# One row of each partition is read with the second load and the last, and one exponential makes its sum

## The chip, the cores and the metric

The kernel runs on one core of a Trainium2 chip. The metric is the device time of one execution in microseconds: 161.43 us as the median of 3 runs (161.34 to 161.46). The profile is one further execution, which took 161.56 us; its span, from the first to the last instruction recorded, is 160.2 us.

## The reference

The input `x` is 32 x 512 x 1024 in fp32 (67.1 MB), of normally distributed numbers. For each of the 16,384 rows of 1024 numbers the result is the logarithm of the sum of their exponentials:

```python
max_x = np.max(x, axis=-1, keepdims=True)
return max_x.squeeze(-1) + np.log(np.sum(np.exp(x - max_x), axis=-1))
```

## The kernel before

The kernel first computes `log(sum(exp(x)))` without taking the maximum off. It then counts whether any sum lies outside 1e-15 to 1e15, and only in that case does everything again with the maximum, inside `nc.If`. With this input that branch isn't taken.

**Rows.** Each of 128 partitions has NC = 128 rows. Rows 0 to 111 (W = 112) of a partition are neighbours in memory (`x_rows`: from one partition to the next it is 112 x 4 KB = 448 KB). The other B = 16 rows come from the end of the input (`x_rest`: 64 KB from one partition to the next). The order of reading is `x_rows`, then `x_rest`.

**Loads.** The list `LOADS` (L22) has 19 loads, counted from 0 here; each entry has its rows for each partition (they need not be whole) and what is done with them. SP issues all of them in order on one queue, into a ring of 48 rows in SBUF (`load`, L137). A load is issued when the sums that read its place in the ring are done. A load that no longer fits starts at the ring's beginning. The first is hoisted to the program's top (`start_early`).

**Work.** ACT waits for a load and writes its exponentials in place (L231), one instruction for each part of the entry. Then come the letters of the list:
- `R9`: DVE sums 9 rows in one reduction (L242).
- `G5`: POOL adds the second half of each of 5 rows to the first (L237); with a later `H`, DVE sums the half rows (`sum_folded`, L161).
- `T4`: DVE sums 4 rows one by one, each with an instruction that adds its halves and accumulates (`add_halves`, L169). At load 15 (`HELD`) DVE also waits for load 16's landing.
- `C`: DVE takes least and total of the sums so far, for the check at the end (`check_early`, L178).
- `L`: ACT takes the early logarithm, of the first 112 sums (L204).
- `a`, `b`: the last row comes in two loads. Part `a` (0.53 row) is added up by DVE into column 127 of `sumexp`; part `b` (480 elements) gets an exponential on ACT that itself accumulates its sum into `rest` (L226).

**End.** SP stores the 112 early results (L265). ACT takes the logarithm of the other 15 whole rows (L269), and then that of the last row, with `rest` as input and DVE's sum as the bias operand (L271). For the latter it waits for the semaphore `parts_summed`, which both parts raise. Then ACT copies `rest` into `sumexp` (L274), SP stores 16 results (L276), DVE checks the sums since `C` (L280, L284), TensorE adds the counts over the partitions in three small matmuls (L290 to L294), the last of them with ACT's copy, and DVE compares (L298). ACT and DVE read that flag and branch. SP waits for both branches and both stores, and ends.

The order of work on each engine is the order in which the Python code issues it, so the list sets it.

Of the kernel before, what the change touches and what calls it, by code (L numbers as in the profile page):

```python
# [11 lines left out]
B = 16  # L12
# [7 lines left out]


LOADS = [  # L22
# [5 lines left out]
]  # L28
# [25 lines left out]
def kernel(  # L54
# [29 lines left out]

    def source(e0, size):
        assert e0 >= W * d or e0 + size <= W * d
        return x_rest[:, e0 - W * d : e0 - W * d + size] if e0 >= W * d else x_rows[:, e0 : e0 + size]

    loads = [
# [5 lines left out]
    assert sum(size for size, _ in loads) == NC * d  # L95

    def sbuf(name, cols, dtype=fp32, rows=P):
        return nc.alloc_sbuf_tensor(name, [rows, cols], dtype).ap()
# [3 lines left out]

    LEAST, TOTAL, REST = NC, NC + 1, NC + 2
    sumexp = sbuf("sumexp", NC + 3)
    res = sbuf("res", NC)
    clamped = sbuf("clamped", NC)
# [5 lines left out]
    count = nc.alloc_psum_tensor("count", [1, 1], fp32).ap()  # L112
    rest = nc.alloc_psum_tensor("rest", [P, 1], fp32).ap()

    unused = nc.alloc_psum_tensor("unused", [P, H], fp32).ap()

    landed = [nc.alloc_semaphore(f"landed{i}") for i in range(len(loads))]
# [7 lines left out]
    ready = nc.alloc_semaphore("ready")  # L125

    parts_summed = nc.alloc_semaphore("parts_summed")
    stored = nc.alloc_semaphore("stored")
# [8 lines left out]
    def load(i, here, done_before, size):  # L137
        for a, b, who, at in users:
            if a < here + size and b > here:
                sp.wait(who, at)  # L140
        assert not any(p0 < here + size and p0 + s * d > here for _, p0, s, _ in folded)
        users[:] = [u for u in users if not (u[0] < here + size and u[1] > here)]
        return nc.sync.dma_start(  # L143
            out=ring[:, here : here + size], in_=source(done_before, size)
        ).then_inc(landed[i], 16)

    c = 0
# [9 lines left out]
    def sum_folded():  # L157
        for c0, p0, s, at in folded:
            dve.wait(pool, at)
            half = ring[:, p0 : p0 + s * d].rearrange("p (c d) -> p c d", d=d)[:, :, 0:H]  # L160
            at = dve.did(nc.vector.reduce_sum(out=sumexp[:, c0 : c0 + s], in_=half, axis=AX.X))  # L161
# [4 lines left out]
    def add_halves(v, col):  # L166
        h = v.shape[-1] // 2
        lo = v[:, 0:h]
        return nc.vector.scalar_tensor_tensor(  # L169
            out=lo, in0=lo, scalar=1.0, in1=v[:, h : 2 * h],  # L170
            op0=ALU.mult, op1=ALU.add, accum_out=sumexp[:, col : col + 1],
        )

# [7 lines left out]

    for i, (size, parts) in enumerate(loads):
        if here + size > RING * d:
            assert here == p
            p = here = 0
        dma = load(i, here, done_before, size)
        first_load = first_load or dma.ins
        end = here + size
        done_before += size
        act.wait(landed[i], 16)  # L190
        for k, part in enumerate(parts):
# [8 lines left out]
            if part[0][0] == "L":  # L200
                assert c >= W
                assert dve.seen[act.sem.num] >= summed_by_act
                act.wait(dve, max(at for c0, _, at in summed if c0 < W))
                ln_early = act.did(nc.scalar.activation(  # L204
                    out=res[:, 0:W], in_=sumexp[:, 0:W], func=AF.Ln
                ))
                continue
# [16 lines left out]
            v = ring[:, here:upto]  # L224
            if part[-1][0] == "b":
                nc.scalar.activation(  # L226
                    out=unused[:, 0 : upto - here], in_=v, func=AF.Exp, accum_out=rest
                ).then_inc(parts_summed, 1)
                here = upto
                continue  # L230
            at = act.did(nc.scalar.activation(out=v, in_=v, func=AF.Exp))  # L231
            here = upto
            for how, s in part:
                rows = ring[:, p : p + s * d].rearrange("p (c d) -> p c d", d=d)
# [5 lines left out]
                elif how == "R":  # L240
                    dve.wait(act, at)
                    users.append((p, p + s * d, dve, dve.did(nc.vector.reduce_sum(  # L242
                        out=sumexp[:, c : c + s], in_=rows, axis=AX.X
                    ))))
                    summed.append((c, c + s, dve.n))
                elif how == "T":
                    if i == HELD:
                        nc.vector.wait_ge(landed[i + 1], 16)
                        nc.vector.nop(nofuse=True)
                    dve.wait(act, at)  # L250
                    for r in range(s):
                        n_sums = dve.did(add_halves(rows[:, r, :], c + r))
                        users.append((p + r * d, p + (r + 1) * d, dve, n_sums))
                        summed.append((c + r, c + r + 1, n_sums))
                elif how == "a":
                    dve.wait(act, at)
                    add_halves(ring[:, p:upto], LAST).then_inc(parts_summed, 1)
                    s = 0
# [4 lines left out]
    assert by_act + sum(c1 - c0 for c0, c1, _ in summed) == LAST  # L263
# [5 lines left out]
    act.did(nc.scalar.activation(out=res[:, W:LAST], in_=sumexp[:, W:LAST], func=AF.Ln))  # L269
    nc.scalar.wait_ge(parts_summed, 2)  # L270
    ln_last = act.did(nc.scalar.activation(  # L271
        out=res[:, LAST:NC], in_=rest, func=AF.Ln, bias=sumexp[:, LAST:NC]
    ))
    last = act.did(nc.scalar.copy(out=sumexp[:, REST : REST + 1], in_=rest))  # L274
    sp.wait(act, ln_last)
    nc.sync.dma_start(out=out_rest, in_=res[:, W:NC]).then_inc(stored, 16)  # L276

    dve.wait(act, summed_by_act)
    nc.vector.wait_ge(parts_summed, 2)
    bads = dve.did(nc.vector.scalar_tensor_tensor(  # L280
# [13 lines left out]
    at = pe.did(nc.tensor.matmul(  # L294
        count, lhsT=ones, rhs=sumexp[:, REST : REST + 1], start=False, stop=True
    ))
# [9 lines left out]
    with nc.If(all_fine < 1):  # L306

        nc.scalar.wait_ge(sp.sem, 16)
        nc.scalar.wait_ge(stored, 16)
# [42 lines left out]
    nc.sync.wait_ge(done, 2)  # L352
    nc.sync.wait_ge(sp.sem, 16)
    nc.sync.sem_clear(range(landed[0].num, stored.num))
# [55 lines left out]
```

## Time and profile before

| | |
|---|---|
| median of 3 runs | 161.43 us |
| the profiled execution | 161.56 us |
| its span | 160.2 us |
| DVE busy | 116.1 us, 72% |
| ACT busy | 114.5 us, 71% |
| POOL busy | 33.3 us, 21% |
| read from memory | 67.11 MB, 419 GB/s over the span |
| exponentials (L231) | 25 of them, 112.2 us |
| row sums on DVE (L242, L161, L169) | 89.8, 16.5 and 9.8 us |

In the lines that follow, L242 is line 242 of the kernel before. A line of the timeline gives start and length in us, engine, line, operation, tiles, shapes and count; a bracket at its end gives how long the engine stood idle before it and what ended that. Neighbours of one kind may be merged, and the length is then theirs together. A group's line ends with busy us, mean ns of one, and idle us before. A line of the DMA issues ends with KB and the us from issue to landing. SPq is SP's queue of issues.

### The profile page before, as it was taken

Reading aid. Unit: us, or ns where it says so; the run is one execution under the profiler, and the core shown is the slowest. Engines: PE = TensorE matmul, PEld = TensorE weight load, DVE = VectorE, ACT = ScalarE, POOL = GpSimd, SP = SyncE. Lnnn points to the kernel's source line nnn. Section 1 sums busy time; section 2 is a strip of 40 time slices with the busy share of each in tenths; the row PEclk is TensorE's granted clock in tenths of the full one; section 3 lists DMA queues with packets and bytes.
Section 4 is the critical chain, followed back from the end, with each engine's and each line's share of the span. In section 5 each row is a group of like instructions: output and inputs, shape, how many; then the busy total and the mean of one; then the engine's idle time right before and its main releaser. Section 6 shows DMA issues by size and latency. Waiting matters only on the chain.

```text
span 160.2 us, 183 instructions
## 1 busy us (share of the span) xinstructions
PE 0.3 (0%) x6; PEld 0.2 (0%) x6; DVE 116.1 (72%) x56; ACT 114.5 (71%) x32; POOL 33.3 (21%) x14
## 2 busy tenths in 40 slices
PE   0000000000000000000000000000000000000000
PEld 0000000000000000000000000000000000000000
DVE  0000000029998499999999799929989999999996
ACT  3000069970899519992799449964998999999996
POOL 0000000000000000000000000990580489996000
DMA  8999799799699699997999999997999999999992
GB/s 288 479 511 431 336 514 450 321 514 497 272 512 512 288 463 478 478 448 312 424 467 467 467 429 429 429 429 332 498 426 409 415 440 394 438 419 425 417 408 101
DMA packets 3025, 67.18 MB, mean 419 GB/s; under 512 B 592, under 2 KB 720, under 8 KB 1488
## 3 DMA queue, kind: packets, MB, share of 16 engines
q1 hardware_dynamic: 3024, 67.18, 97.9%
q14 instruction: 1, 0.01, 0.0%
HBM read 67.11 MB, written 0.07 MB: 419 GB/s over the span
## 4 chain that ended last, share of the span: by engine, by line
DMA 54%; DVE 21%; ACT 19%; POOL 5%; issue 0%; PE 0%; SPq 0%
DMA ring<-in_x_dram 54%; ACT ring L231 19%; DVE sumexp L242 15%; POOL ring L237 5%; DVE ring L169 3%; DVE sumexp L161 2%; SPq L143 0%; DVE clamped L280 0%; PE count L290 0%; ACT res L204 0%; DVE fine L298 0%; PE count L292 0%; PE count L294 0%
## 5 line engine op out<-in xcount | busy, mean ns | idle before, releaser
L231 ACT ACTIVATE ring<-ring 128x16000 f32<-128x16000 f32 (+24 forms) x25 | 112.2, 4546 | 42.8 <-DMA ring<-in_x_dram 42.8
L242 DVE TENSOR_REDUCE sumexp<-ring 128x9 f32<-128x9216 f32 (+7 forms) x10 | 89.8, 9000 | 39.2 <-ACT ring L231 39.2
L237 POOL TENSOR_TENSOR ring<-ring 128x2048 f32<-128x2048 f32 (+5 forms) x8 | 33.0, 4135 | 112.3 <-ACT ring L231 112.3
L161 DVE TENSOR_REDUCE sumexp<-ring 128x4 f32<-128x2048 f32 (+5 forms) x8 | 16.5, 2080 | 3.5 <-POOL ring L237 3.5
L169 DVE SCALAR_TENSOR_TENSOR ring<-ring 128x512 f32<-128x512 f32 (+1 forms) x16 | 9.8, 671 | 0.0
L130 ACT ACT_TABLE_LOAD x1 | 1.3, 1283 | 1.4 <-PEq L63 1.4
L169 DVE DVE_READ_ACCUMULATOR ring<-ring 128x1 f32 x16 | 1.3, 82 | 0.0
L226 ACT ACTIVATE unused<-ring 128x480 f32<-128x480 f32 x1 | 0.6, 559 | 0.0
L290 PE MATMUL count<-far,bad 128*1 128x1 f32 x2 | 0.2, 164 | 158.7 <-DVE clamped L280 158.7
L178 DVE TENSOR_REDUCE sumexp<-sumexp 128x1 f32<-128x106 f32 x2 | 0.4, 258 | 0.0
L298 DVE TENSOR_SCALAR fine<-count 1x1 int32<-1x1 f32 x1 | 0.1, 146 | 0.3 <-PE count L294 0.3
L131 POOL MEMSET ones<- 128x1 f32 x1 | 0.1, 98 | 1.0 <-POOLq L63 1.0
L290 PEld LDWEIGHTS count<-far,bad 128*1 128x1 f32 x2 | 0.1, 80 | 158.7 <-DVE clamped L280 158.7
L204 ACT ACTIVATE res<-sumexp 128x112 f32<-128x112 f32 x1 | 0.3, 279 | 0.0
L271 ACT ACTIVATE res<-rest,sumexp 128x1 f32<-128x1 f32 x1 | 0.3, 261 | 0.0
L280 DVE SCALAR_TENSOR_TENSOR clamped<-sumexp 128x23 f32<-128x23 f32 x1 | 0.2, 183 | 0.0
L269 ACT ACTIVATE res<-sumexp 128x15 f32<-128x15 f32 x1 | 0.2, 205 | 0.0
L292 PE MATMUL count<-total,ones 128*1 128x1 f32 x2 | 0.2, 164 | 0.0
L294 PE MATMUL count<-sumexp,ones 128*1 128x1 f32 x2 | 0.2, 164 | 0.0
L284 DVE TENSOR_REDUCE total<-sumexp 128x1 f32<-128x24 f32 x1 | 0.2, 173 | 0.0
L274 ACT COPY sumexp<-rest 128x1 f32<-128x1 f32 x1 | 0.2, 152 | 0.0
L394 POOL MEMSET const-float32-0.0<- 128x1 f32 x1 | 0.1, 98 | 0.2 <-issue 0.2
(8 smaller groups left out, 0.8 us busy)
## 6 DMA issues: line engine op xcount, KB each, us to landing
ring<-in_x_dram SPq DMA_DIRECT2D x1, 8048.0 KB, 39.1
ring<-in_x_dram SPq DMA_DIRECT2D x1, 8016.0 KB, 57.6
ring<-in_x_dram SPq DMA_DIRECT2D x1, 8000.0 KB, 21.5
ring<-in_x_dram SPq DMA_DIRECT2D x1, 7472.0 KB, 25.8
ring<-in_x_dram SPq DMA_DIRECT2D x1, 7312.0 KB, 22.9
ring<-in_x_dram SPq DMA_DIRECT2D x1, 6720.0 KB, 21.5
ring<-in_x_dram SPq DMA_DIRECT2D x1, 5200.0 KB, 17.6
ring<-in_x_dram SPq DMA_DIRECT2D x1, 3584.0 KB, 19.1
```

Of the source, the lines that this page charges most:

```text
L130: nc.scalar.preload_act_table_set("natural_log_exp_and_others")
L161: at = dve.did(nc.vector.reduce_sum(out=sumexp[:, c0 : c0 + s], in_=half, axis=AX.X))
L169: return nc.vector.scalar_tensor_tensor(out=lo, in0=lo, scalar=1.0, in1=v[:, h : 2 * h], op0=ALU.mult, op1=ALU.add, accum_out=sumexp[:, co ...
L178: dve.did(nc.vector.tensor_reduce(out=sumexp[:, col : col + 1], in_=sumexp[:, 0:c], op=op, axis=AX.X))
L204: ln_early = act.did(nc.scalar.activation(out=res[:, 0:W], in_=sumexp[:, 0:W], func=AF.Ln))
L226: nc.scalar.activation(out=unused[:, 0 : upto - here], in_=v, func=AF.Exp, accum_out=rest).then_inc(parts_summed, 1)
L231: at = act.did(nc.scalar.activation(out=v, in_=v, func=AF.Exp))
L237: folded.append((c, p, s, pool.did(nc.gpsimd.tensor_tensor(out=rows[:, :, 0:H], in0=rows[:, :, 0:H], in1=rows[:, :, H:d], op=ALU.add,))))
L242: users.append((p, p + s * d, dve, dve.did(nc.vector.reduce_sum(out=sumexp[:, c : c + s], in_=rows, axis=AX.X))))
L269: act.did(nc.scalar.activation(out=res[:, W:LAST], in_=sumexp[:, W:LAST], func=AF.Ln))
L271: ln_last = act.did(nc.scalar.activation(out=res[:, LAST:NC], in_=rest, func=AF.Ln, bias=sumexp[:, LAST:NC]))
L290: pe.did(nc.tensor.matmul(count, lhsT=bad, rhs=far, start=True, stop=False))
```

## The change

The reading order is turned round: first `x_rest` (16 rows), then `x_rows` from the middle of its row 15 to its end, and last `x_rows` from its beginning up to that point. So row 15 of each partition's `x_rows` is split: its second part of 544 elements (`EARLY`) stands at the head of load 1, and its first part of 480 elements (`TAIL`) is the whole of load 18, the last.

- DVE sums the 544 early exponentials into column W = 112 of `sumexp`; later rows move up a column (`column`). The early logarithm `L` covers 113 columns and writes into `edge`, with that logarithm at the end of them.
- The last load no longer goes to the ring but to the places of `edge` right behind that logarithm. SP issues it after the early logarithm, with its wait. One exponential over 481 elements (the logarithm and the 480 numbers) then accumulates the whole row's sum into `whole`. The last logarithm has that alone as input, with no bias operand, and waits for ACT itself.
- The row before it, row 14 of `x_rows`, is read in the two loads before the last. Part `c` (0.5625 row) is added up by DVE into `in_part_sum`, part `a` (0.4375 row) by a DVE instruction that hasn't been used before in this kernel, `tensor_tensor_reduce`, with `in_part_sum` as its start value. The logarithm of 15 rows waits for it.
- The list has new cuts. Again there are 19 loads. The first three hold 16, 15.625 and 15.906 rows, the last 480 elements as before. POOL folds 25 rows in place of 29. `C` moves from load 8 to load 3.
- The early results go out in two stores in place of one (16 and 96 results), behind the last load in SP's queue.

```diff
 LOADS = [
-    (15.625, "R15"), (15.71875, "R16"), (15.65625, "R9 R7"), (14.59375, "R14"),
-    (14.28125, "G7 H R7"), (13.125, "G5 H R9"), (10.15625, "G4 H R3+G3 H"), (7, "G4 R2 H G1"),
-    (5.84375, "H C G2+R1 G3 H"), (4.46875, "T4"), (3.09375, "T3 L"), (2.40625, "T2"),
-    (1.75, "T2"), (1.25, "T1"), (0.75, "T1"), (0.65625, "T1"), (0.625, "T1"), (0.53125, "a"),
-    (0.46875, "b"),
+    (16, "R16"), (15.625, "R15"), (15.90625, "R16"), (15.21875, "C R15"), (15.8125, "R10 G6 H"),
+    (12.96875, "R7 G6"), (9.25, "R5 G4 H"), (7.25, "G4 R3 H"), (4.5, "G3 H G1 H G1 H"),
+    (4.125, "T4"), (2.96875, "T3 L"), (2.3125, "T2"), (1.71875, "T2"), (1.25, "T1"),
+    (0.9375, "T1"), (0.6875, "T1"), (0.5625, "c"), (0.4375, "a"), (0.46875, "b"),
 ]
...
+    def pieces(e0, size):
+        for start, end, at in (
+            (0, B * d, x_rest),
+            (B * d, W * d + EARLY, x_rows[:, (B - 1) * d + TAIL : W * d]),
+            (W * d + EARLY, NC * d, x_rows[:, 0 : (B - 1) * d + TAIL]),
+        ):
+            if start <= e0 and e0 + size <= end:
+                return at[:, e0 - start : e0 - start + size]
...
+    edge = sbuf("edge", B - 1 + W + 1 + TAIL)
+    early = edge[:, B - 1 : B + W]
...
             at = act.did(nc.scalar.activation(out=v, in_=v, func=AF.Exp))
             here = upto
+            if head is not None:
+                dve.wait(act, at)
+                sums = dve.did(nc.vector.reduce_sum(
+                    out=sumexp[:, W : W + 1], in_=ring[:, head : head + EARLY], axis=AX.X
+                ))
...
+                elif how == "c":
+                    dve.wait(act, at)
+                    in_part = add_halves(ring[:, p:upto], in_part_sum)
...
                 elif how == "a":
+                    dve.wait(dve, in_part)
                     dve.wait(act, at)
-                    add_halves(ring[:, p:upto], LAST).then_inc(parts_summed, 1)
+                    sums = dve.did(nc.vector.tensor_tensor_reduce(
+                        out=lo, in0=lo, in1=ring[:, middle + h : upto], scale=1.0, scalar=in_part_sum,
+                        op0=ALU.add, op1=ALU.add, accum_out=sumexp[:, LAST : LAST + 1],
+                    ))
...
     sp.wait(act, ln_early)
-    nc.sync.dma_start(out=out_rows, in_=res[:, 0:W]).then_inc(sp.sem, 16)
+    nc.sync.dma_start(
+        out=edge[:, B + W : B + W + TAIL], in_=pieces(done_before, TAIL)
+    ).then_inc(landed[-1], 16)
+    nc.sync.dma_start(out=out_rest, in_=early[:, 0:B]).then_inc(sp.sem, 16)
+    nc.sync.dma_start(out=out_rows[:, B:W], in_=early[:, B:W]).then_inc(sp.sem, 16)
+    act.wait(landed[-1], 16)
+    in_whole = act.did(nc.scalar.activation(
+        out=unused[:, 0 : TAIL + 1], in_=edge[:, B + W - 1 : B + W + TAIL], func=AF.Exp,
+        accum_out=whole,
+    ))
 
     sums = dve.n
     act.wait(dve, sums)
-    act.did(nc.scalar.activation(out=res[:, W:LAST], in_=sumexp[:, W:LAST], func=AF.Ln))
-    nc.scalar.wait_ge(parts_summed, 2)
-    ln_last = act.did(nc.scalar.activation(
-        out=res[:, LAST:NC], in_=rest, func=AF.Ln, bias=sumexp[:, LAST:NC]
-    ))
-    last = act.did(nc.scalar.copy(out=sumexp[:, REST : REST + 1], in_=rest))
+    act.did(nc.scalar.activation(out=late[:, 0 : B - 1], in_=sumexp[:, W + 1 : NC], func=AF.Ln))
+    act.wait(act, in_whole)
+    ln_last = act.did(nc.scalar.activation(out=late[:, B - 1 : B], in_=whole, func=AF.Ln))
+    last = act.did(nc.scalar.copy(out=sumexp[:, WHOLE : WHOLE + 1], in_=whole))
```

More of the change, by code (lines that the diff above doesn't have):

```diff
@@ L202 @@
                 assert dve.seen[act.sem.num] >= summed_by_act
-                act.wait(dve, max(at for c0, _, at in summed if c0 < W))
+                act.wait(dve, max(at for c0, _, at in summed if c0 <= W))
                 ln_early = act.did(nc.scalar.activation(
-                    out=res[:, 0:W], in_=sumexp[:, 0:W], func=AF.Ln
+                    out=early, in_=sumexp[:, 0 : W + 1], func=AF.Ln
                 ))
@@ L224 @@
             v = ring[:, here:upto]
[L225 to L230, printed above, removed]
             at = act.did(nc.scalar.activation(out=v, in_=v, func=AF.Exp))
             here = upto
+            if head is not None:
[3 more added lines that the diff above has]
+                ))
+                users.append((head, head + EARLY, dve, sums))
+                summed.append((W, W + 1, sums))
+                head = None
             for how, s in part:
```

64 lines of the change are left out of this document (42 added, 22 removed).

## The prediction

> **What bounds the kernel now.** I read the page's DMA lines first.
>
> ```profile
> span 160.2 us, 183 instructions
> ...
> q1 hardware_dynamic: 3024, 67.18, 97.9%
> ```
>
> One queue moves all 67 MB, and its packets fill 97.9% of sixteen engines' span. The chain of waits shows where that stream ends the run and where it does not (start, length, what):
>
> ```profile
> 119.72 23.78 DMA ring<-in_x_dram
> 143.50 0.02 issue
> 143.52 6.75 ACT ring L231 x2
> ...
> 156.74 1.74 DVE ring L169 x7
> ```
>
> Up to 143.50 the chain is loads and what frees their space; behind it stand ACT and then DVE. But the last loads belong beside them. The issues of the last two from SP's timeline (start, length), and from the DMA issues the times to landing of the last two loads and the two stores:
>
> ```profile
> 134.59 4.56 SPq L143 DMA_DIRECT2D ring<-in_x_dram  x1
> 139.19 3.71 SPq L143 DMA_DIRECT2D ring<-in_x_dram  x1
> ```
>
> ```profile
> ring<-in_x_dram SPq DMA_DIRECT2D x1, 272.0 KB, 22.6
> ring<-in_x_dram SPq DMA_DIRECT2D x1, 240.0 KB, 18.6
> out_dram<-res SPq DMA_DIRECT2D x1, 56.0 KB, 7.5
> out_dram<-res SPq DMA_DIRECT2D x1, 8.0 KB, 1.4
> ```
>
> 134.59 + 22.6 = 157.2 and 139.19 + 18.6 = 157.8. The end, from the timelines of ACT, DVE and SP:
>
> ```profile
> 155.99 1.92 ACT L231 ACTIVATE ring<-ring 128x672 f32<-128x672 f32 x3
> 157.82 0.56 ACT L226 ACTIVATE unused<-ring 128x480 f32<-128x480 f32 x1
> 158.31 0.13 ACT L226 ACTIVATION_READ_ACCUMULATOR unused<-ring 128x1 f32 x1
> 158.36 0.20 ACT L269 ACTIVATE res<-sumexp 128x15 f32<-128x15 f32 x1
> 158.50 0.26 ACT L271 ACTIVATE res<-rest,sumexp 128x1 f32<-128x1 f32 x1
> 158.66 0.15 ACT L274 COPY sumexp<-rest 128x1 f32<-128x1 f32 x1
> ```
>
> ```profile
> 158.01 0.44 DVE L169 SCALAR_TENSOR_TENSOR ring<-ring 128x272 f32<-128x272 f32 x1
> 158.38 0.08 DVE L169 DVE_READ_ACCUMULATOR ring<-ring 128x1 f32 x1
> ```
>
> ```profile
> 158.78 0.34 SPq L276 DMA_DIRECT2D out_dram<-res  x1
> ```
>
> Three things meet within 0.1 us: the last load lands at 157.8, ACT leaves the exponential before it at 157.91, and the last exponential starts at 157.82 (two of ACT's instructions overlap by some 0.09). DVE's share of the last row is summed at 158.46, ACT's at 158.44; the last logarithm (L271) needs both. Its store leaves at 158.78 and needs 1.4 us: 160.2, the span. So the time is the stream (157.8) plus 2.4 us of tail. The profiled execution took 161.56 us, 0.13 above the median of 161.43; I sum differences against it and take them off the median.
>
> **The stream.** Bytes and number of loads (19) stay. ACT's timeline gives its pace, by the exponentials that start as their load lands (loads 3, 4, 5, 6, 8, 9), and SP's the issue of load 6:
>
> ```profile
> 77.09 12.66 ACT L231 ACTIVATE ring<-ring 128x14944 f32<-128x14944 f32 x1 [3.98 <-DMA ring<-in_x_dram]
> 94.34 12.48 ACT L231 ACTIVATE ring<-ring 128x6560 f32<-128x6560 f32 x2 [4.60 <-DMA ring<-in_x_dram]
> 110.25 11.50 ACT L231 ACTIVATE ring<-ring 128x4224 f32<-128x4224 f32 x2 [3.42 <-DMA ring<-in_x_dram]
> 122.53 15.22 ACT L231 ACTIVATE ring<-ring 128x4096 f32<-128x4096 f32 x5 [0.79 <-DMA ring<-in_x_dram]
> 138.08 5.28 ACT L231 ACTIVATE ring<-ring 128x2912 f32<-128x2912 f32 x2 [0.33 <-DMA ring<-in_x_dram]
> 143.52 4.02 ACT L231 ACTIVATE ring<-ring 128x4576 f32<-128x4576 f32 x1 [0.16 <-DMA ring<-in_x_dram]
> ```
>
> ```profile
> 104.89 0.33 SPq L143 DMA_DIRECT2D ring<-in_x_dram  x1
> ```
>
> Load 4 has 14.28 rows a partition and took 94.34 - 77.09 = 17.25 us, 1.208 a row. The last 16 rows took 157.8 - 138.08 = 19.7 us, 1.23 a row: 0.4 us more than 16 x 1.208. I put that on the ten small loads' own cost, since 5.44 us for the 4.47 rows of load 9 is still 1.217. The same sum then holds with the new cuts: the last load again lands at 157.8, if the queue never runs dry.
>
> It runs dry when a load is issued after the one ahead of it has landed. Load 6 has the least room now: issued at 104.89, while load 5 lands at 110.25, 5.4 us ahead. For the new list I need durations, from the groups by form of single engines in short stretches (last columns: busy us, mean ns, idle before), and one row of POOL's timeline:
>
> ```profile
> L242 DVE TENSOR_REDUCE sumexp<-ring 128x16 f32<-128x16384 f32 x1 | 17.2, 17220 | 2.9 <-ACT ring L231 2.9
> L242 DVE TENSOR_REDUCE sumexp<-ring 128x1 f32<-128x1024 f32 x1 | 1.2, 1208 | 0.0
> L169 DVE SCALAR_TENSOR_TENSOR ring<-ring 128x512 f32<-128x512 f32 x1 | 0.7, 692 | 0.0
> L169 DVE SCALAR_TENSOR_TENSOR ring<-ring 128x272 f32<-128x272 f32 x1 | 0.4, 437 | 0.0
> L231 ACT ACTIVATE ring<-ring 128x16000 f32<-128x16000 f32 x1 | 13.5, 13536 | 18.8 <-DMA ring<-in_x_dram 18.8
> L226 ACT ACTIVATE unused<-ring 128x480 f32<-128x480 f32 x1 | 0.6, 559 | 0.0
> L271 ACT ACTIVATE res<-rest,sumexp 128x1 f32<-128x1 f32 x1 | 0.3, 261 | 0.0
> L269 ACT ACTIVATE res<-sumexp 128x15 f32<-128x15 f32 x1 | 0.2, 205 | 0.0
> L237 POOL TENSOR_TENSOR ring<-ring 128x512 f32<-128x512 f32 x1 | 1.3, 1274 | 0.0
> ```
>
> ```profile
> 143.44 3.44 POOL L237 TENSOR_TENSOR ring<-ring 128x1536 f32<-128x1536 f32 x1 [0.29 <-ACT ring L231]
> ```
>
> ACT: (13536 - 559)/15520 = 0.836 ns an element and 0.16 us each (0.18 for the small ones: three of 672, 640 and 544 fill 155.99 to 157.91, 1.92 = 1856 x 0.836 ns + 0.37, so each adds some 0.1 to its elements, overlap taken off). DVE sums: (17220 - 1208)/15360 = 1.042 ns and 0.14. Row by row at 1.208, loads 0 to 6 now land at 22.0, 40.9, 60.1, 78.5, 97.6, 113.3, 124.4. Load 3 needs the space of R16: 22.0 + 13.9 (exp) + 17.2 (sum) = 53.1, and load 2 lands at 60.1, 7.0 ahead. Load 4 needs R15: exp until 54.4, half row (0.7) and sum (16.2): 71.3 against 78.5. Load 5: R16 from 73.9 to 91.2 against 97.6. Load 6: R15 until 107.9 against 113.3, 5.4 ahead. Load 7: R10 until 118.6 against 124.4. Later loads are over 14 ahead. No margin is under the present smallest, so the new half-row sum (0.7 us) and the early check, which moves here from load 8 (two sums over 47 columns, 0.4 us), cost nothing; what hides them is this 5 to 7 us of queued transfers, past which they would cost in full.
>
> **The last load's new wait.** It is now issued after the early logarithm. That needs row 112's sum (DVE's first add of load 9) and ACT's place behind load 10. Load 7 lands at 133.2 with ACT free; its exponentials and those of load 8 (3840, 3584, 2560, 1024, 1024 elements), one behind the other, end at 136.6, 139.8, 142.0, 142.9 and 143.9. POOL folds load 8's rows from 142.1 (three in 3.44, one in 1.27, one in 1.27) until 148.0; DVE's sum of the last one (0.68) and its first add (0.69) end by 149.4. ACT, with loads 9 and 10 (7264 elements), is through at 150.2, the logarithm of 113 at 150.4; that decides. Load 17 lands at 157.2: 6.8 us of queue cover the issue, against the 1.4 us that a small transfer takes. Behind that wait stand only the two early stores and the last store, so nothing else is late. Two early stores in place of one of 56 KB drain behind the last load and before 158.7.
>
> **ACT's end.** Loads 9 to 17 hold 15,360 elements in place of 15,904. From 143.9, 15,360 x 0.836 ns = 12.8 us, nine times that 0.1 some 0.87, the logarithm 0.19: 157.76, where it was 157.91. It can then start at 157.66, so the landing alone decides: 157.82 again, gain nothing.
>
> **The tail.** The exponential over 481 elements and its read cost what 480 did: 158.44. DVE's new instruction for part `a` is not in this trace. The add of 272 elements took 437 ns, and (692 - 437)/240 = 1.06 ns an element makes 0.39 us for 224. The upper end is POOL's fold of one row, 1.27 us. I take 0.39, the same kind of work on the same engine. It waits for load 17's exponential (157.76) and for part `c`. DVE's 14 adds of rows 112 to 125, from 148.6 on and 0.61 apart (0.69 less 0.08 overlap), with small waits for their exponentials, end at 157.4; `c`, 288 elements, 0.45 more, 157.8. So `a` runs from 157.84 to 158.24, and the logarithm of 15 could not start before 158.36 anyway: some 0.09 us is spare. The last logarithm no longer waits for DVE (158.46): from ACT's own read 158.44 it gains 0.02. It also loses its bias operand: 15 elements without one took 0.205 us (L269), less 14 x 0.836 ns is 0.19 for one, against 0.26 (L271): gain 0.07. The bounds of that edit are nothing and 0.26.
>
> [...]
>
> Store, copy, matmul and check all hang on that logarithm or the copy behind it, and move together: DVE's checks (L280, 82 elements instead of 23, some 0.06 us more) now start at 158.27 and stay ahead. **Sum: 0.02 + 0.07 = 0.09 us.** 161.56 becomes 161.47 in a profile, the median 161.43 becomes 161.34. A difference under 0.2%, 0.32 us, is about what a measurement of this kernel cannot tell from none.
>
> **The rivals.**
> - *DVE's new instruction is dear* (slower). Over 0.48 us it holds the logarithm of 15 and all behind it; from 0.57 the time passes today's. At POOL's 1.27 us it is 161.34 + 0.79 = 162.1; at 0.61 (448 elements one by one at 1.042 ns, and 0.14) 161.47. For it: no row shows it, and only 0.09 is spare. Against it: DVE's other sums all run near 1.04 ns an element. 0.14, half of it over the bound.
> - *Small loads cost more where rows lie 448 KB apart* (the last 16 rows now come from there, not from the rows 64 KB apart). If the surplus of 0.4 us doubles: 161.74. Against it: 1.208 a row for big loads there. 0.10, over half of it beyond the bound.
> - *The reverse*: the surplus belonged to the 64 KB rows, not to small loads; read as one big load it goes: 160.94. Against it: load 9 at 1.217. 0.10, faster.
> - *The first load, 16 rows at a 64 KB pitch in sixteen parallel streams, runs slowly.* At the pace of today's last loads (0.6 us for 0.469 rows, from 157.2 to 157.8 at 1.28 a row) it costs 16 x 0.07 = 1.15 us, nothing of which is hidden: 162.5. Against it: load 9 read the same pitch without loss. 0.04.
> - *It does not do what it says*: the logarithm of 15 still waits for DVE's share, and 0.09 is lost again: 161.43. 0.04.
>
> [...]
>
> **How the numbers follow.** Forecast 0.58, with 0.15 us around it for the three-way tie at 157.8. Faster by over 0.2%: the reverse case, 0.10. Slower: 0.07 + 0.06 + 0.04 = 0.17. Within: 0.73. The range leaves out the reverse case, the slow first load and the dearest end of the DVE case, together about 0.19: 161.05 to 161.9.
>
> **What would show it.** Right: the last exponential starts at 157.8 with a wait on DMA ahead of it; the last logarithm takes 0.19 us and starts 0.03 behind ACT's read; the store leaves at 158.7. Wrong: the 128x224 DVE instruction over 0.5 us; ACT busy without a gap into the last exponential; the first exponential later than 22.1; more than 1.25 us a row in the last 16 rows; an idle slice in DMA's line before the end.

## The result, and the profile after

The changed kernel took **162.11 us** (median of 6 runs, 161.99 to 162.26); the kernel before took 161.50 in the 6 runs it has by now (161.34 to 161.67). The ratio is 1.0038, interval 1.0025 to 1.005: slower by 0.4%. The forecast was 161.34 with a range to 161.9; both missed. The profiled execution took 162.14 us, 0.58 more than before's 161.56, where I had expected 0.09 less.

First the page of after: span, and the DMA queues.

```profile
span 160.6 us, 181 instructions
...
q1 hardware_dynamic: 3168, 67.18, 97.7%
```

The stream still fills the span, and the instruction queue of before's page (`q14 instruction: 1, 0.01, 0.0%`, one packet) has no line here. Nothing in this page says "slower" but the span; the place has to be found at the end. ACT's timeline there (start, length):

```profile
157.34 0.58 ACT L254 ACTIVATE ring<-ring 128x448 f32<-128x448 f32 x1
157.95 0.57 ACT L318 ACTIVATE unused<-edge 128x481 f32<-128x481 f32 x1
158.46 0.13 ACT L318 ACTIVATION_READ_ACCUMULATOR unused<-edge 128x1 f32 x1
158.56 0.21 ACT L325 ACTIVATE late<-sumexp 128x15 f32<-128x15 f32 x1
158.68 0.15 ACT L327 ACTIVATE late<-whole 128x1 f32<-128x1 f32 x1
158.73 0.15 ACT L328 COPY sumexp<-whole 128x1 f32<-128x1 f32 x1
```

DVE beside it:

```profile
158.06 0.45 DVE L298 CUSTOM_DVE_ANT_0 ring<-ring,in_part_sum 128x224 f32<-128x224 f32 x1 [0.16 <-ACT ring L254]
158.44 0.08 DVE L298 DVE_READ_ACCUMULATOR2_ANT sumexp<- 128x1 f32 x1
158.56 0.24 DVE L334 SCALAR_TENSOR_TENSOR clamped<-sumexp 128x82 f32<-128x82 f32 x1
158.73 0.23 DVE L338 TENSOR_REDUCE total<-sumexp 128x1 f32<-128x83 f32 x1
159.29 0.15 DVE L352 TENSOR_SCALAR fine<-count 1x1 int32<-1x1 f32 x1 [0.33 <-PE count L348]
```

And SP's last store, with its time to landing from the DMA issues (KB, us):

```profile
158.86 0.33 SPq L330 DMA_DIRECT2D out_dram<-late  x1
```

```profile
out_dram<-late SPq DMA_DIRECT2D x1, 8.0 KB, 1.4
```

The last exponential starts at 157.95 in place of 157.82, the store leaves at 158.86 in place of 158.78 and lands 1.4 us later, as before. So the results are in memory only 0.06 us later (160.257 for 160.193). The other 0.5 us lies behind that, in instructions that count as no work. DVE reads the flag (`values_load`, a TENSOR_LOAD) and branches (`nc.If`, a COMPARE_BRANCH). The rows of these source lines have the duration in ns (shortest, median, longest) and first and last start. Before:

```profile
L301 DVEq TENSOR_LOAD <-fine x1: 540/540/540, 159.3 to 159.3; - x1
```

```profile
L351 DVEq COMPARE_BRANCH  x1: 72/72/72, 159.9 to 159.9; - x1
```

After:

```profile
L355 DVEq TENSOR_LOAD <-fine x1: 544/544/544, 159.5 to 159.5; - x1
```

```profile
L405 ACTq COMPARE_BRANCH  x1: 45/45/45, 160.0 to 160.0; - x1
...
L405 DVEq COMPARE_BRANCH  x1: 72/72/72, 160.5 to 160.5; - x1
```

Both loads of the flag take 0.54 us. Before's branch follows 0.08 us behind its load (159.834 to 159.910 in the trace), after's 0.50 us (160.025 to 160.526), although ACT's branch on the same flag came at 160.0. The span now ends with DVE's branch (160.60), no longer with SP (160.23 before, 160.31 now).

**How the end counts.** In 19 of the 20 profiled executions of this study the time is, within 0.01 us, the larger of two sums: SP's end + 1.336, and DVE's end + 1.540. Before: 160.226 + 1.336 = 161.56, and DVE's 159.982 + 1.540 = 161.52. After: SP 161.64, DVE 160.598 + 1.540 = 162.14. The 0.58 us are then, along DVE's path: 0.134 for the later last exponential, 0.053 from there to the flag's load, 0.425 for the longer wait ahead of the branch, and off that the 0.04 by which DVE's path was the shorter one before.

### The profile page after: what moved, and what is told of

Read it like the earlier page. It is cut to its first block, busy times and chain, and to the rows that moved or that the text cites. A ratio compares the mean times of both kernels' runs of the same rounds, so it can differ in the third digit from the quotient of the medians.

```text
span 160.6 us, 181 instructions
## 1 busy us (share of the span) xinstructions
PE 0.4 (0%) x6; PEld 0.2 (0%) x6; DVE 118.6 (74%) x54; ACT 114.6 (71%) x31; POOL 28.7 (18%) x13
## 4 chain that ended last, share of the span: by engine, by line
DMA 38%; ACT 32%; DVE 28%; PE 0%; issue 0%; DVEq 0%
DMA ring<-in_x_dram 38%; ACT ring L254 32%; DVE sumexp L273 27%; DVE ring L298 0%; DVE clamped L334 0%; PE count L344 0%; ACT edge L233 0%; PE count L346 0%; DVE fine L352 0%; PE count L348 0%; DVEq L53 0%; DVE sumexp L298 0%
## 5 line engine op out<-in xcount | busy, mean ns | idle before, releaser
L254 ACT ACTIVATE ring<-ring 128x1024 f32<-128x1024 f32 (+22 forms) x24 | 112.3, 4732 | 42.8 <-DMA ring<-in_x_dram 42.8
L273 DVE TENSOR_REDUCE sumexp<-ring 128x16 f32<-128x16384 f32 (+5 forms) x8 | 93.8, 11748 | 38.7 <-ACT ring L254 38.7
L268 POOL TENSOR_TENSOR ring<-ring 128x3072 f32<-128x3072 f32 (+3 forms) x7 | 28.4, 4072 | 117.9 <-ACT ring L254 117.9
L185 DVE TENSOR_REDUCE sumexp<-ring 128x6 f32<-128x3072 f32 (+3 forms) x7 | 14.1, 2052 | 0.1
L193 DVE SCALAR_TENSOR_TENSOR ring<-ring 128x512 f32<-128x512 f32 (+1 forms) x15 | 9.2, 672 | 0.2 <-ACT ring L254 0.2
L258 DVE TENSOR_REDUCE sumexp<-ring 128x1 f32<-128x544 f32 x1 | 0.7, 719 | 1.4 <-ACT ring L254 1.4
L318 ACT ACTIVATE unused<-edge 128x481 f32<-128x481 f32 x1 | 0.6, 575 | 0.0
L298 DVE CUSTOM_DVE_ANT_0 ring<-ring,in_part_sum 128x224 f32<-128x224 f32 x1 | 0.5, 452 | 0.2 <-ACT ring L254 0.2
```

Of the source, the lines that this page charges most:

```text
L185: at = dve.did(nc.vector.reduce_sum(out=sumexp[:, k : k + s], in_=half, axis=AX.X))
L193: return dve.did(nc.vector.scalar_tensor_tensor(out=lo, in0=lo, scalar=1.0, in1=v[:, h : 2 * h], op0=ALU.mult, op1=ALU.add, accum_out=to,))
L258: sums = dve.did(nc.vector.reduce_sum(out=sumexp[:, W : W + 1], in_=ring[:, head : head + EARLY], axis=AX.X))
L268: folded.append((c, p, s, pool.did(nc.gpsimd.tensor_tensor(out=rows[:, :, 0:H], in0=rows[:, :, 0:H], in1=rows[:, :, H:d], op=ALU.add,))))
L298: sums = dve.did(nc.vector.tensor_tensor_reduce(out=lo, in0=lo, in1=ring[:, middle + h : upto], scale=1.0, scalar=in_part_sum, op0=ALU.add ...
L318: in_whole = act.did(nc.scalar.activation(out=unused[:, 0 : TAIL + 1], in_=edge[:, B + W - 1 : B + W + TAIL], func=AF.Exp, accum_out=whole,))
```

## The experiments

**Theory.** The wait ahead of the branch comes from where it stands in DVE's program. By my count of the compiled program DVE has 80 instructions before and 79 after; the trace, which leaves 15 of them out in every run, lists 65 and 64, the branch as the last. My conjecture: at one fixed place in that program the 8 KB packet of the instruction queue (8192 bytes in the traces of before and after; the fetch, below) is called for, and a branch that stands first behind that place pays for it in full at the very end. **Rival:** something in the change itself (the new instruction, the three-engine check) makes the branch late. What pointed to the theory at the start is the DMA throughput of the end, in GB/s by slices of 0.2 us from 155 on (before, then after):

```profile
GB/s 414 410 408 405 403 415 392 401 415 366 280 122 18 0 0 41 0 0 0 0 0 0 0 40 1 0 0 0 0 0 0 0 0 0 0 0 0 0 0 0
```

```profile
GB/s 361 428 392 358 382 405 380 371 410 339 288 198 83 4 0 0 0 0 0 0 0 0 0 31 10 0 0 0 0 0 0 41 0 0 0 0 0 0 0 0
```

Behind the stream two things of 8 KB each remain: the last store (from 159.6 in both) and the packet of the instruction queue. Before has it at 158.0, between the stream and the store; after has it at 161.2, behind everything.

### Instructions that do nothing, put into one engine's program

```diff
+        if i == 1:
+            for _ in range(1):
+                nc.vector.wait_ge(landed[0], 16)
+                nc.vector.nop(nofuse=True)
         act.wait(landed[i], 16)
```

The wait has long been satisfied when DVE comes to it; the wait with its nop is one instruction more. In the table, "load to branch" is the time from the end of the flag's load to DVE's branch, and "fetch at" the start of the 8 KB packet of the instruction queue. This is e1; e4 has two of them, e5 eight, and in e2 ACT gets the one, as a control.

> The changed kernel with one more instruction in DVE's program: a wait for load 0, long satisfied, before DVE's second sum; DVE has over a microsecond spare there. Theory A (the loss of 0.6 us lies mostly at the very end, in how DVE's program reaches its branch: the branch starts 0.50 us behind the flag's load instead of 0.08, and a block of instructions is fetched after the span instead of before its end; the program is one DVE instruction shorter, so the place of the branch in it has moved): gap back to 0.08 us, the span ends with SP at about 160.3, time about 161.6, ratio to before 1.000 to 1.002. Rival B (the loss is the later landing of the last load, 157.93 for 157.78, and what follows from it; the branch is a symptom): the nop changes nothing, time 162.1, ratio 1.004.

> The same extra wait in ACT's program instead of DVE's, a control. ACT's program too is one instruction shorter than before. Theory A: DVE's gap stays at 0.50 us and the time at 162.1 (ratio 1.004). If ACT's place is what matters: about 161.6. Rival B: 162.1.

> The changed kernel with two more waits in DVE's program at the same place. Theory A: the branch lies behind the edge of the block by one more instruction, gap 0.08 us, time about 161.6 as with one. Rival B: 162.1.

> The changed kernel with eight satisfied waits at the place where the earlier runs had one and two. With one and two the branch gap was back at 0.08 us, but the block of instructions came at 159.4 to 159.5, between the last store's issue and its landing, and the store took 1.85 us for 1.4. Theory A2 (one place in DVE's program, the same in all kernels, starts the fetch when DVE's queue reads up to it; what counts is when that happens against the last store): eight instructions move that place ahead of the wait of the new sum, so the fetch comes near 158.0, behind the stream and ahead of the store, as in the kernel before. Gap 0.08, store 1.40 us, time 161.6 to 161.75, ratio 1.001 to 1.002. Rival B2 (the store is late for another reason, such as the two early stores): store 1.85 us again, time 162.2.

| run | DVE's instructions | load to branch | fetch at | store to landing | time | ratio to before |
|---|---|---|---|---|---|---|
| after | 79 | 0.50 | 161.21 | 1.40 | 162.11 | 1.0038 (1.0025 to 1.005) |
| e2, ACT + 1 | 79 | 0.50 | 161.51 | 1.40 | 162.31 | 1.0049 (1.0036 to 1.0063) |
| e1, DVE + 1 | 80 | 0.07 | 159.53 | 1.88 | 162.39 | 1.0058 (1.0044 to 1.0072) |
| e4, DVE + 2 | 81 | 0.08 | 159.41 | 1.85 | 162.25 | 1.0056 (1.0043 to 1.007) |
| e5, DVE + 8 | 87 | 0.08 | 158.29 | 1.40 | 161.83 | 1.0019 (1.001 to 1.0028) |

One instruction more in DVE's program takes the wait away, and one in ACT's does not. But e1 and e4 gained nothing by it: their store lands later. The throughput of e1 in the same slices shows what has moved:

```profile
GB/s 405 405 371 385 389 396 393 366 399 334 267 186 47 20 0 0 0 0 0 0 0 0 41 0 40 1 0 0 0 0 0 0 0 0 0 0 0 0 0 0
```

The fetch now runs from 159.53 on, right ahead of the store's packets (159.82 to 160.03), and takes 0.41 us. Of the store's sixteen increments of the semaphore fifteen came between 160.27 and 160.40 and the last at 160.88. The store's packets themselves are recorded in 0.21 us, as in after. That the fetch ahead of them delays the last increment is argued from the two standing together in e1 and e4; how it could is not shown. With eight more instructions the fetch falls to 158.3, ahead of the store's issue, and the store takes 1.4 us again. That is 0.28 us faster than after.

### The same edge in the kernel before, and one instruction less in after

```diff
-                    if i == HELD:
-                        nc.vector.wait_ge(landed[i + 1], 16)
-                        nc.vector.nop(nofuse=True)
```

e3 takes DVE's held wait at load 15 out of the kernel before (79 instructions), e9 does the same and adds the satisfied wait at load 1 (80), e10 takes the held wait out of after (78).

> The kernel before without the wait for load 16's landing ahead of load 15's row (HELD), so DVE's program is one instruction shorter, as long as in the changed kernel; nothing else changes. Theory A: DVE's branch starts 0.5 us behind the flag's load, the span grows to about 160.6, time about 162.0 to 162.1, ratio 1.003 to 1.004. Rival B: the hold does no work at the end, time 161.5, ratio 1.000.

> The kernel before, with its held wait at load 15 taken out of DVE's program and one satisfied wait put in at load 1. DVE's program has 80 instructions, as before. Theory (the place of the last branch in DVE's program counts, not the wait): DVE's gap between the end of its TENSOR_LOAD and its COMPARE_BRANCH is 0.08 us as in before, and the time is before's, 161.5 us, within 0.2%. Rival (the held wait itself keeps something away from the end): the gap stays near 0.49 us and the time near 161.85, as in the kernel before without it.

> The changed kernel without its held wait; DVE's program has 78 instructions, one less than after's. Theory (a fixed edge in the program: the gap is paid only when the branch is the first instruction behind the edge): the branch now stands ahead of it, the gap falls to 0.08 us and the time to 161.6 to 161.8, unless what follows the branch then waits in its place, in which case DVE's end stays 0.4 us late and the time near 162.1. Rival (every program that is shorter than 80 pays): the gap stays at 0.42 to 0.50 us and the time at 162.1.

The branch rows of e3, e9 and e10:

```profile
L348 DVEq COMPARE_BRANCH  x1: 72/72/72, 160.3 to 160.3; - x1
```

```profile
L352 DVEq COMPARE_BRANCH  x1: 72/72/72, 159.9 to 159.9; - x1
```

```profile
L402 DVEq COMPARE_BRANCH  x1: 67/67/67, 160.2 to 160.2; - x1
```

- e3: 0.49 us from load to branch, 161.85 us (1.0027, 1.0018 to 1.0037). The kernel before, without a line of the change, gets the same wait by losing one instruction. The rival falls.
- e9: 0.08 us, 161.53 (1.0008, 0.9999 to 1.0017). What the held wait was worth here, it was worth as one more instruction.
- e10: 0.07 us, yet 162.16 us (1.0043, 1.0029 to 1.0057). It is the one execution that the rule of the two ends misses: DVE's end 160.232 + 1.540 = 161.77, but it took 162.17. The branch now stands ahead of the place in the program where the wait fell (the edge of the heading), and 0.40 us come behind it, outside the span; the fetch is at 161.34. Moving the branch ahead of the edge moves the cost, and does not remove it.

All four programs of 79 (after, e2, e3 and e6) show 0.49 to 0.50 us, the fifteen of 80 to 87 show 0.07 or 0.08. So the number of DVE's instructions decides. What DVE waits for in those 0.42 us is not shown: in the four programs of 79 the 8 KB packet starts 0.67 to 0.69 us after the branch (161.21 against 160.53 in after), and no packet at all is recorded between the end of the flag's load and the branch. That the packet and the wait are two signs of one cause is an argument. What calls for the packet, and why it comes earlier in the longer programs (158.03 in before, 158.29 in e5), is not shown either. What the runs show is that a place in DVE's program costs time: 0.42 us ahead of the branch with 79 instructions, 0.40 us behind it with 78.

### Which piece of the input the small loads read

e6 swaps the pieces: loads 0 and 2 to 8 read `x_rows`, and the small loads `x_rest`, as in before. e8 is e6 with the eight waits of e5.

```diff
-            (0, B * d, x_rest),
-            (B * d, W * d + EARLY, x_rows[:, (B - 1) * d + TAIL : W * d]),
-            (W * d + EARLY, NC * d, x_rows[:, 0 : (B - 1) * d + TAIL]),
+            (0, B * d, x_rows[:, 0 : B * d]),
+            (B * d, B * d + EARLY, x_rest[:, (B - 1) * d + TAIL : B * d]),
+            (B * d + EARLY, W * d + EARLY, x_rows[:, B * d : W * d]),
+            (W * d + EARLY, NC * d, x_rest[:, 0 : (B - 1) * d + TAIL]),
```

> The changed kernel with the roles of the two pieces of the input exchanged: the split row and the last loads come from the rows 64 KB apart (as the last 16 rows did before), the first loads from the rows 448 KB apart. Load 1 needs two transfers for it, and one early store goes out in place of two. Theory S (small loads cost more where rows lie 448 KB apart): the last ten loads take 19.1 us for 15.47 rows in place of 19.3, last landing about 0.15 earlier relative to the first. Rival (the cuts themselves cost it): 19.3 again. DVE's program keeps its length, so the branch gap stays 0.50 and the time is 162.0 under the first, 162.15 under the second.

> The exchange of the two pieces and the eight waits together, which is a full kernel. If theories S and A2 both hold: time about 161.45, ratio 0.999 to 1.001. If only A2: 161.65.

e6 took 162.09 us (1.0038, 1.0024 to 1.0052): as after. Its last ten loads, from the landing of load 8 to that of load 18, took 19.28 us; after's took 19.30, for 0.531 row fewer than before's 19.73. Before's 19.73 less that half row at the prediction's 1.208 us a row is 19.09, so 0.2 us are lost, and not through the 448 KB between the rows. e8 took 161.68 (1.0016, 1.0006 to 1.0025). It differs from e6 by the eight waits alone, so these are worth 0.41 us in a full kernel.

### DVE's new instruction

e7 sums part `a` with the ordinary add of halves. It leaves out the first 576 numbers of row 14 of each partition, as the start value is lost; two satisfied waits keep DVE's program at 80.

```diff
-                    dve.wait(dve, in_part)
                     dve.wait(act, at)
-                    sums = dve.did(nc.vector.tensor_tensor_reduce(
...
-                    ))
+                    sums = add_halves(ring[:, middle:upto], sumexp[:, LAST : LAST + 1])
```

> The changed kernel with part a summed by the same add instruction as part c, without the start value and its extra wait; it leaves out the first 576 numbers of one row of each partition. Two satisfied waits keep DVE's program at the length of the kernel before. Theory A2: nothing stops DVE's queue behind part c, so the fetch comes near 158.0, gap 0.08, store 1.40. The logarithm of 15 no longer waits for DVE: 0.06 us earlier than in the changed kernel relative to the last landing. Time about 161.6 to 161.7. Rival B2: store 1.85, time 162.1.

```profile
158.09 0.58 ACT L316 ACTIVATE unused<-edge 128x481 f32<-128x481 f32 x1
158.61 0.13 ACT L316 ACTIVATION_READ_ACCUMULATOR unused<-edge 128x1 f32 x1
158.66 0.20 ACT L323 ACTIVATE late<-sumexp 128x15 f32<-128x15 f32 x1
```

The logarithm of 15 now starts 0.05 us behind ACT's read, as in before; in after it was 0.10. From the last exponential's start to the store's issue it is 0.867 us, against 0.965 before and 0.906 after. The time is 161.69 us (1.0013, 1.0004 to 1.0022), with a last load that landed at 158.07 in the profile.

### The 0.2 us of the small loads

What was left was the stream. The trace's records of single packets show a difference that no group shows: in before every packet of 1920 bytes takes 79.0 ns, in after 85.7 on average with a standard deviation of 5.9, and so for all packets from load 14 on (2304 bytes: 97.1, deviation 4.1). Six runs left it where it was, or did not bring it about. e11 gives before the new cuts of loads 13 to 17:

```diff
-    (1.75, "T2"), (1.25, "T1"), (0.75, "T1"), (0.65625, "T1"), (0.625, "T1"), (0.53125, "a"),
+    (1.75, "T2"), (1.1875, "T1"), (0.9375, "T1"), (0.6875, "T1"), (0.5625, "T1"), (0.4375, "a"),
```

e12 is e8 with the last load issued ahead of SP's wait for the logarithm; ACT waits for that instead:

```diff
-    sp.wait(act, ln_early)
     nc.sync.dma_start(
         out=edge[:, B + W : B + W + TAIL], in_=pieces(done_before, TAIL)
     ).then_inc(landed[-1], 16)
+    sp.wait(act, ln_early)
...
+    act.wait(act, ln_early)
     act.wait(landed[-1], 16)
```

e13 is e8 with load 6 and those behind it three rows further on in the ring; e14 (on e8) and e15 (on before) shift them by six:

```diff
-            p = here = 0
+            p = here = 3 * d if i == 6 else 0
```

e17 is e8 with ACT held until load 17 has landed:

```diff
+        if i == 14:
+            act.wait(landed[17], 16)
```

> The kernel before with loads 13 to 17 cut as in the changed kernel (1.1875, 0.9375, 0.6875, 0.5625, 0.4375 rows in place of 1.25, 0.75, 0.65625, 0.625, 0.53125); nothing else is changed. If the new cuts cost the stream its 0.2 us, the last ten loads take 19.95 us in place of 19.73 and the last load lands near 158.0, time 161.7. If they don't: 19.73, 157.8 and 161.5.

> The kernel with the two pieces of the input swapped and eight satisfied waits in DVE (161.68 us, last load landed at 157.89), with the last load issued as soon as SP comes to it, ahead of the wait for the early logarithm; ACT waits for that logarithm instead. If the late issue, or what it does to the queue, costs the stream its 0.2 us, the last ten loads take 19.1 us in place of 19.3, the last load lands at 157.7 and the time is 161.5, at most before's. If not: 19.3 us, 157.9 and 161.7.

> The kernel with the two pieces of the input swapped and eight satisfied waits in DVE, with loads 6 to 17 put three rows further on in the ring, so that loads 14 to 17 go to rows 36.4 to 39 of it in place of 33.4 to 36; before's go to 36 to 39. Theory (the place in the ring decides how fast the small loads are written): their packets go back to the even times of before (79 ns for 1920 bytes in place of 86), the last ten loads take 19.15 us in place of 19.31, and the time falls from 161.68 to about 161.55. Rival (the place does not matter): 86 ns, 19.3 us, 161.68.

> The same with six rows in place of three (loads 14 to 17 at rows 39.4 to 42). By the theory of the place: other packet times than at 33.4 to 36, even ones if the slow stretch is a narrow one. By the rival: 86 ns, 19.3 us and 161.68 once more.

> The kernel before with loads 6 to 18 six rows further on in the ring (loads 14 to 18 at rows 42 to 45 in place of 36 to 39). By the theory of the place the packets of 1920 bytes may leave their 79.0 ns without any spread, and the last ten loads their 19.73 us, by up to 0.2. By the rival nothing changes: 79 ns, 19.73 us, 161.5.

> The same kernel (without the new starts), with ACT held at load 14 until load 17 has landed, so that ACT works on nothing while loads 16 to 18 are written; the end is later by some 2 us for it. Theory (ACT's work beside the writing slows the small packets): the packets of 1792 and 1920 bytes go back to 74 and 79 ns without spread. Rival (ACT has no part in it): 77 and 86 ns as before the hold.

| run | time | ratio to before | last ten loads | 1920 bytes: mean ns, deviation |
|---|---|---|---|---|
| before | 161.50 | | 19.73 | 79.0, 0 |
| e11 | 161.54 | 1.0007 (0.9998 to 1.0016) | 19.61 | 79.0, 0 |
| e15 | 165.60 | 1.026 (1.0246 to 1.0274) | 19.74 | 79.0, 0 |
| e8 | 161.68 | 1.0016 (1.0006 to 1.0025) | 19.31 | 85.0, 5.8 |
| e12 | 161.73 | 1.0016 (1.0007 to 1.0025) | 19.29 | 85.9, 5.5 |
| e13 | 161.75 | 1.0016 (1.0007 to 1.0025) | 19.27 | 85.5, 5.6 |
| e14 | 169.57 | 1.0505 (1.0491 to 1.0519) | 19.27 | 85.5, 5.7 |
| e17 | 164.03 (one run) | | 19.26 | 85.8, 5.5 |

Neither the cuts, nor the late issue, nor whole rows of place in the ring, nor ACT's work beside the writing decides. (The sum over ten loads itself scatters: e9, with before's loads, had 19.89. The packets are the sharper sign, and so is the sum of the last five loads: 4.09 us in after and 3.85 in e11 for the same 3.09 rows.) e14 and e15 cost 8 and 4 us for a reason that has nothing to do with the packets, which the throughput by slices of the span (e14: 4.2 us each) shows at once:

```profile
GB/s 281 468 499 499 250 537 471 471 294 425 496 496 388 357 475 475 475 445 276 493 493 493 247 493 518 405 202 0 271 433 433 357 452 398 441 422 422 414 409 115
```

Load 6 (9.25 rows), put at row 6 of the ring, reaches to 15.25, and the ten rows that DVE sums with load 4 begin at 15 (the first part of them came with load 3). For a quarter of a row it waits for a whole sum: issued at 118.57 in place of e8's 107.72, while load 5 landed at 113.08, and the queue runs dry (in e15 load 6 is issued at 111.68, and load 5 had landed at 109.98).

Then the starts of the loads within a row. Counted from the start of a row, loads 10 and 13 to 18 of after start at multiples of 256 bytes, and 11 and 12 do not; 11 and 12 are those whose packets have no spread (9472 bytes: 356.0 ns, 7040: 267.0). Loads 14 to 18 of e11, with after's cuts and no spread, all start off those multiples. e16 is e8 with the starts of loads 10 to 17 moved by 128 bytes (their places in the ring move with them):

```diff
-    (4.125, "T4"),
+    (4.15625, "T4"),
...
-    (0.5625, "c"), (0.4375, "a"),
+    (0.5625, "c"), (0.40625, "a"),
```

e18 turns that round: in before, the starts of loads 10 to 17 move to multiples of 256.

```diff
-    (4.46875, "T4"), (3.09375, "T3 L"), (2.40625, "T2"),
+    (4.5, "T4"), (3.0625, "T3 L"), (2.4375, "T2"),
...
-    (0.65625, "T1"),
+    (0.625, "T1"),
```

> The kernel with the two pieces of the input swapped and eight satisfied waits in DVE, with load 9 longer by 1/32 row (4.15625) and load 17 shorter by it (0.40625): loads 10 to 17 then start 128 bytes later, at odd multiples of 128 bytes within the row or nearly so, as several of before's small loads do, in place of multiples of 256. Theory (the starts decide): loads 14 to 16 lose the spread of their packets (2304 bytes in 93.0 ns in place of 97) and the last ten loads take 19.15 us in place of 19.31. Rival (the starts do not matter): 97 ns with its spread, 19.3 us, 161.68.

> The kernel before with loads 9 to 11 and 15 cut by 1/32 row differently (4.5, 3.0625, 2.4375, 0.625), so that loads 10 to 17 all start at multiples of 256 bytes within the row, as in the changed kernel; only load 18 keeps its start. It is the last run's edit turned round. Theory (the starts decide): its packets get a spread that before's have not (2560 bytes in more than 102 ns, 2176 in more than 88), and the last ten loads take up to 0.2 us more than 19.73; the time is 161.5 to 161.7. Rival (what the odd starts took away was due to something else in the changed kernel): no spread, 19.73 us, 161.47.

e16: 161.58 us (1.0008, 0.9999 to 1.0017), last ten loads 19.06 us. Packets of 2304 bytes take 93.0 ns (95.0 in e8, deviation 3.8) and of 1920 bytes 79.0, without any deviation; those of loads 11 and 12, which now start at multiples of 256, have one (3.0 and 2.0 ns). The last five loads take 3.86 us for 3.06 rows, where e8's took 4.08 for 3.09. e18: 161.66 us (1.0012, 1.0003 to 1.0021), 19.97 us; 2560 bytes take 105.9 ns in place of 102.0, 2176 bytes 91.1 in place of 88.0, with deviations of 3.9 and 3.7. The windows from 153 to 157 us, with GB/s in their last column, point the same way, but less clearly (before, after, e8, e16, e18): e8, from which e16 was made, is nearer to before than to after.

```profile
153.00:157.00 4.00, 0.00 (x0) 0.00 (x0) 3.96 (x13) 4.00 (x5) 0.00 (x0) 1.00 1.02 402
```

```profile
153.00:157.00 4.00, 0.00 (x0) 0.00 (x0) 3.81 (x13) 4.00 (x5) 0.00 (x0) 1.00 1.03 395
```

```profile
153.00:157.00 4.00, 0.00 (x0) 0.00 (x0) 3.81 (x13) 4.00 (x5) 0.00 (x0) 1.00 1.03 401
```

```profile
153.00:157.00 4.00, 0.00 (x0) 0.00 (x0) 3.88 (x15) 4.00 (x5) 0.00 (x0) 1.00 1.03 406
```

```profile
153.00:157.00 4.00, 0.00 (x0) 0.00 (x0) 3.88 (x13) 4.00 (x5) 0.00 (x0) 1.00 1.03 396
```

So the starts switch the spread on and off in both kernels. What that is worth in time is less certain: e18 took 0.21 us more than before in its own comparison (161.45), e16 took 0.10 less than e8, and their intervals overlap. The places in the ring move with the starts, so whether the place in memory or the one in SBUF counts is not separated. How they do it stays open: before's loads 11, 16 and 17 and e16's load 18 start at multiples of 256 too, and have no spread, so it is not a matter of one load alone. In this stretch of small loads the starts at multiples of 256 were the slower ones (2304 bytes: 95.0 ns in e8 and 97.1 in after against 93.0 in e16).

No version beats the kernel before. With both costs taken away (e16) the changed kernel cannot be told from it, though the interval only just reaches 1. Two things of the change are still in e16: the logarithm of 15 starts 0.14 us behind ACT's read, held by the new instruction (0.05 in e7), and DVE's end still closes the run, 160.163 + 1.540 = 161.70 against SP's 161.63. No run takes all three costs away and is a full kernel.

## Why the prediction was wrong

- **The end of the run: wrong.** The failed step is "Store, copy, matmul and check all hang on that logarithm or the copy behind it, and move together", on top of "the time is the stream plus 2.4 us of tail". It followed the store alone to the end. DVE's path to its branch was only 0.04 us shorter than SP's in before and decides now. I counted instructions that were added and removed by their durations, and never counted how many DVE has; one fewer put 0.42 us ahead of its branch (0.41 in the time, from e8 to e6), a term that the prediction had at nothing. No rival had it. The 162.1 at the dear end of the rival on the new instruction matches the 162.11 by accident: that instruction took 0.452 us, not 1.27.
- **"DVE's checks stay ahead": wrong, and worth 0.05 us.** They started at 158.56, not 158.27, since the new instruction ended at 158.52, not 158.24. Behind it the two checks, longer by 0.06 us each, lay on the path to the flag: they ended at 158.96, ACT's copy at 158.88 (158.78 and 158.81 in before).
- **The stream: wrong by 0.15 us in the profile.** "The last load again lands at 157.8"; it landed at 157.93 (157.84 to 158.23 in the other runs with after's cuts and no shift). The rival for it named the distance between the rows; e6 rules that out; e16 and e18 point to the starts of the loads. The first load came at 21.83 us against 22.0 in my table, so that rival fell, too.
- **The queue's room: right.** Loads 0 to 6 landed at 21.83, 40.72, 59.94, 78.33, 97.41, 113.08 and 124.31, each within 0.25 us of the forecast; no load kept the queue waiting, and the late issue of the last one (150.28, forecast 150.4) cost nothing, as e12 shows. Where e14 took the margin away, load 6 waited for the sum that the prediction ended at 118.6 (118.49 in that run), and the time rose by the 8 us of a dry queue.
- **The tail's gain of 0.09 us: right in size, not collected.** The last logarithm took 0.152 us, 0.109 less than before (0.07 forecast). In e7 and e12, where DVE does not hold ACT up, it took 0.171, 0.090 less. Both are more than the 70 ns that my rows gave. e7 gains 0.098 between the exponential and the store. In after 0.04 of that is lost again on ACT's path, which waits for DVE: the new instruction took 0.452 us (0.39 forecast) and started 0.14 us behind the exponential it waits for, with a semaphore wait of its own ahead of it (e7's add: 0.03). The rival "dear" had its price too high, and its place right.

## What to carry to other kernels

Find every engine whose end closes the run, not only the store's, and by how little the second one is behind. At a tie of 0.04 us the instruction count of the other engine can decide: where a program ends in a branch, count its instructions before and after a change, and when the time moves by some 0.4 us with no work to show for it, look at the gap ahead of the branch and for the instruction queue's packet at the end. A few satisfied waits early in the program tell within one run whether it is that.

## What the runs showed of the hardware that I had not expected

- With 79 instructions for DVE its last branch came 0.42 us later than with 80; with 78 the execution took 0.40 us more behind the branch. In both the instruction queue's last packet, of 8 KB, came behind the branch. Where that packet came 0.3 us ahead of the last store's packets (e1, e4), the store landed 0.45 to 0.48 us later; where it came before the store's issue, the store was not later.
- In 19 of 20 profiles the execution's time was the larger of SP's end + 1.336 us and DVE's end + 1.540 us.
- In a run of small loads that start at multiples of 256 bytes within the row, packets of 2304 bytes took 95.0 ns (e8) and 97.1 (after), unevenly; with the starts, and the places in SBUF with them, moved by 128 bytes (e16) they all took 93.0.
